# Pairing the chunk inverses, moving one page pool, and giving one chain priority in a hybrid encoder layer

## The chip, the core and the metric

The kernel runs on one core of one Trainium2 chip. It computes one layer of a streaming encoder for one sequence of 1024 frames with 1024 channels, in float32. The metric is the device time of one execution in microseconds (us). Three timed runs of the kernel before the change took 1260.48, 1262.43 and 1262.86 us; the median is 1262.43 us. A fourth execution was profiled; it took 1258.55 us, of which 1256.3 us lie between the first and the last recorded instruction.

## The reference, cut to what matters

```python
u    = rms_norm(h, mix_norm_gain)
proj = u @ w_in            # columns: attention q,k,v | delta q,k,v | gate | decay, beta
# A: band attention: 16 chunks of 64 frames, own chunk and 8 past, 8 heads of 64
q, k = rms_norm(q, q_gain), rms_norm(k, k_gain)          # per head
p    = softmax(q @ k.T * 64**-0.5 + rel_bias, masked)
o_att = rms_norm(p @ v, att_out_gain)
# B: gated delta rule: 4 heads of 128, chunks of 64 frames
t_mat = strict_lower((k*beta) @ k.T * decay) + I
value, k_cum = solve(t_mat, v*beta), solve(t_mat, k*beta*exp(decay))
for each chunk:                                          # state S is 128 x 128 per head
    v_new = value - k_cum @ S
    o     = q_decay @ S + attn_intra @ v_new
    S     = S * chunk_decay + k_tail.T @ v_new
o_dn = rms_norm(o, dn_out_gain) * silu(gate)
h = h + concat(o_att, o_dn) @ w_out
h = h + relu(rms_norm(h, ffn_gain) @ w_ff1)**2 @ w_ff2   # 1024 -> 4096 -> 1024
```

## The kernel before, in words

**Arithmetic.** Every large matrix product is made of three products of halves: an operand is split into a high part in a reduced format (`_h`) and the rest (`_l`). ScalarE (ACT) casts the high part, VectorE (DVE) or GpSimd (POOL) subtracts it (`split`, L202 to L204). The two FFN products use a Strassen-like scheme of seven products per block.

**Stages.** (1) The delta keys' projection, then the other projections in the order delta q, delta v, gate, attention keys (tiles `ak`), attention queries (`aq`), attention values (`av`); beside them runs `delta_prep`, which builds the strictly lower matrices of 8 chunks of 128 frames, sends them to DRAM (`a_dr`) and inverts their 32x32 diagonal blocks by a chain of 31 short DVE steps (L595, L599). (2) The mixer: 32 units of attention (two groups of four heads, 8 tiles of 128 frames, two pairs of heads) woven together with the delta rule. (3) The output projection (tiles `op`, `wo`). (4) `ff1`: eight blocks of seven products each (tiles `q`, L1348). (5) `ff2`: four blocks of seven products (tiles `p`, L1444).

**The attention keys' chain.** `att_proj` makes one tile of 128 frames by 24 matmuls into a PSUM bank (`ps_a`, three banks). ACT squares it (L473), DVE sums the squares (L475), then follow scale and eps (L187, DVE), a power of -0.5 (L189, POOL), one Newton step (L192, L194, L195, DVE), the row scale (L477) and the normalised tile `ak_n` (L480, DVE), which frees the bank. TensorE (PE) transposes it (L485), and it is split into `ak_h` and `ak_l`, the latter in the page pool `dk`.

**The inverses.** `delta_low` (L617) joins the 32x32 inverses to 64x64 ones for four chunks; `delta_merge` (L660) joins two 64x64 inverses of one chunk (tile `l_w`) to a 128x128 inverse (`m_yb`). It loads a 64x64 block of `a_dr` per head into `m_sa` (DMA, L667), lets POOL clear and copy parts of `m_yb` (L668 to L670), and then PE makes four 64x64 transposes (L675) and four 64x64 products (L677, eight recorded instructions), ACT copies the result to `m_sa` (L680), PE makes four more 64x64 products (L685), and ACT writes them negated to `m_yb` (L688). PSUM comes from the two banks of `ps_d`, which the whole delta rule shares. A chunk's `m_yb` is used by the product `c_pv` (L516) of `delta_state`, behind `c_pk` of the state. `delta_all` (L813) hands out the work in groups: group c holds the state step of chunk c, the output step of chunk c-1 and the merge of chunk c+2.

**What sets the order.** The mixer is written by a planner: a model clock with costs per engine decides which piece is issued next (`attention`, L831). This gives program order, which is also priority. The framework then runs the program through a model of the chip, and each engine's queue takes the ready instruction of the highest priority; inside `tc.high_priority()` an instruction goes ahead of the rest. The order found is fixed in the program. `held` (L610) issues a first matmul and makes the others follow it at high priority. On the chip every engine works through its queue in that order and waits where an operand is not there; loads are issued by SP's queue.

**Pages.** On-chip memory is cut into pools of equal pages; a tile takes a page of its pool, and when all are taken it waits until an older tile is released. In one pool, pages are handed out in the order of the program. Pool `pp` (7 pages) holds the inverses and, before the change, `m_sa`. Pool `dk` (8 pages) holds the low parts of keys and queries (`ak_l`, `aq_l`), then in program order the four key pages of the first group's first half (`ks`), the value pages `vt` 0 and 1, two key pages of the second half, later four key pages of the second group, and last the low parts of the output projection's left operand.

In the FFN the pools of `ff1` and `ff2` lie over each other: both stacks begin at the same address, and a page of `ff2` can be written once the `ff1` tiles at that address have been read for the last time. Counted in pages of 4 KB from that address, by the addresses of the program before:

| | w0 | h | l | ub11 | ub21 | ut1 | ut2 | ub22 | ut3 | ut4 | w |
|---|---|---|---|---|---|---|---|---|---|---|---|
| ff1 | 0-1 | 2-3 | 4-5 | 6-9 | 10-13 | 14-17 | 18-21 | 22-25 | 26-29 | 30-33 | 34-39 |

| | s1 | hB | r | hA | lA | rc | r2 | lB | y7 |
|---|---|---|---|---|---|---|---|---|---|
| ff2 | 0-1 | 2-5 | 6-13 | 14-17 | 18-21 | 22-27 | 28-35 | 36-39 | 40-41 |

A pool's first tile takes its first page, the second its last, the third the last but one, and so on. In `ff1`, `ub11` ... `ut4` hold the split right operands; each block multiplies them in the order b11, b21, t1, t2, b22, t3, t4; `h` and `l` hold the split left operands of the products at work, and in the last block page 4 holds the low part for t3, page 5 that for t4. In `ff2`, pool `r` holds the loads `a11` and `b11` (first product, `p1`), `rc` the loads `a21`, `a22`, `b12` (needed by the second, `p5`), `r2` those of the third; `s1` holds sums that DVE computes for `p5` (L1522); `hA`, `lA`, `hB`, `lB` hold the splits, A for the first, third, fifth product, B for the others. `p5` of the first block is at high priority.

## Time and profile before

| what | value |
|---|---|
| median of three timed runs | 1262.43 us |
| profiled execution, its own time | 1258.55 us |
| its span, first to last instruction | 1256.3 us |
| PE busy | 1236.3 us, 98% of the span |
| DVE, ACT, POOL busy | 74%, 44%, 22% |
| granted TensorE clock, mean | 0.998 |
| PE busy from 361 to 537 us, the mixer | 169.63 of 176 us |
| PE busy from 633 to 957 us, ff1 up to the first stall of ff2 | 321.22 of 324 us |

A row of the timeline gives the start, the busy time, the engine, the line of the kernel, the operation, `out<-in` by tile names without their numbers, the shapes and the count; what stands in square brackets is the idle time of the engine before it and what ended it. Consecutive instructions of one kind are put together, so "x4, 0.41" is four instructions in 0.41 us. Matmul ends are modelled and each overlaps the next, so the distance between two starts is the better measure of what a matmul occupies.

### The profile page before, as it was taken

Reading aid. Unit: us, or ns where it says so; the run is one execution under the profiler, and the core shown is the slowest. Engines: PE = TensorE matmul, PEld = TensorE weight load, DVE = VectorE, ACT = ScalarE, POOL = GpSimd, SP = SyncE. Lnnn points to the kernel's source line nnn. Section 1 sums busy time; section 2 is a strip of 40 time slices with the busy share of each in tenths; the row PEclk is TensorE's granted clock in tenths of the full one; section 3 lists DMA queues with packets and bytes.
Section 4 is the critical chain, followed back from the end, with each engine's and each line's share of the span. In section 5 each row is a group of like instructions: output and inputs, shape, how many; then the busy total and the mean of one; then the engine's idle time right before and its main releaser. Section 6 shows DMA issues by size and latency. Waiting matters only on the chain.

```text
span 1256.3 us, 17942 instructions
## 1 busy us (share of the span) xinstructions
PE 1236.3 (98%) x6686; PEld 1032.1 (82%) x6686; DVE 932.9 (74%) x1417; ACT 548.1 (44%) x899; POOL 270.5 (22%) x458
## 2 busy tenths in 40 slices
PE   9999999999999999899999999999999999999997
PEld 8778888788889988778888788888887888888886
DVE  7899987755237568776269766767769997997988
ACT  7233132232246756655365444454444543333330
POOL 4425552253133444523200000000000000000043
PEclk9999999999999999999999999999999999999999
DMA  7214364665585633045243333333269614333002
GB/s 228 63 41 141 101 164 118 119 161 134 168 259 136 189 85 88 24 135 176 76 143 104 114 118 118 119 132 101 84 205 365 202 67 134 105 97 101 1 34 100
DMA packets 134374, 158.52 MB, mean 126 GB/s; under 512 B 31120, under 2 KB 78224, under 8 KB 133776
## 3 DMA queue, kind: packets, MB, share of 16 engines
q1 hardware_dynamic: 116192, 135.11, 35.6%
q10 hardware_dynamic: 18096, 22.29, 5.2%
q8 instruction: 52, 0.85, 0.3%
q14 instruction: 34, 0.28, 0.1%
HBM read 109.91 MB, written 47.45 MB: 125 GB/s over the span
## 4 chain that ended last, share of the span: by engine, by line
PE 55%; DVE 5%; ACT 1%; issue 1%; POOL 0%; DVEq 0%; ACTq 0%
PE p L1444 24%; PE q L1348 21%; PE op L222 7%; PE t_o L1026 1%; DVE h L1290 1%; PE t_sa L927 0%; DVE q_0a_l L204 0%; PE t_tpb L987 0%; PE t_tpa L1003 0%; PE t_sb L927 0%; PE c_pv L516 0%; ACT t_pb L966 0%; PE c_po L516 0%; PE t_tpo L520 0%; PE c_pq L516 0%
## 5 line engine op out<-in xcount | busy, mean ns | idle before, releaser
L1516 POOL TENSOR_TENSOR y<-y,y 128x1024 f32<-128x1024 f32 x4 | 11.5, 2890 | 575.7 <-DVE y L1512 570.6
L1512 DVE TENSOR_TENSOR y<-y,p 128x1024 f32<-128x1024 f32 x46 | 55.1, 1217 | 5.4 <-PE p L1444 4.5
L222 PE MATMUL op<-ml,wo_h 128*128 128x512 f32 x128 | 50.2, 395 | 0.0
L222 PE MATMUL op<-mh,wo_h 128*128 128x512 f32 x128 | 49.2, 394 | 0.8 <-ACT mh L203 0.8
L222 PE MATMUL op<-mh,wo_l 128*128 128x512 f32 x128 | 49.3, 391 | 0.0
L947 DVE CUSTOM_DVE_ANT_0 t_pb<-t_sb,biasn 128x256 f32<-128x256 f32 (+1 forms) x64 | 23.2, 401 | 31.4 <-PE t_sb L927 31.3
L966 ACT ACTIVATE t_pb<-t_pb,t_nm 128x256 f32<-128x256 f32 (+1 forms) x64 | 31.4, 491 | 17.2 <-DVE t_nm L958 15.5
L1229 DVE TENSOR_TENSOR h<-op,op_x 128x512 f32<-128x512 f32 x16 | 10.8, 686 | 29.2 <-PE op L222 29.2
L1236 POOL TENSOR_TENSOR op_q<-op_q 128x512 f32<-128x512 f32 x14 | 19.6, 1400 | 55.4 <-ACT op_q L1235 55.1
L222 PEld LDWEIGHTS op<-mh,wo_h 128*128 128x128 f32 x128 | 23.9, 188 | 6.4 <-ACT mh L203 1.2
L222 PEld LDWEIGHTS op<-ml,wo_h 128*128 128x128 f32 x128 | 24.1, 188 | 5.0 <-DVE ml L204 0.2
L222 PEld LDWEIGHTS op<-mh,wo_l 128*128 128x128 f32 x128 | 24.1, 188 | 5.0
L958 DVE CUSTOM_DVE_ANT_0 t_pa<-t_sa,biaso,t_nm 128x384 f32<-128x384 f32 (+2 forms) x48 | 24.9, 543 | 2.8 <-PE t_sa L927 1.6
L970 ACT ACTIVATE t_pa<-t_pa,t_nm 128x384 f32<-128x384 f32 (+2 forms) x48 | 26.5, 552 | 0.0
L222 PE MATMUL aq_ps<-waq_h,ul 128*128 128x512 f32 x64 | 25.5, 399 | 0.0
L222 PE MATMUL dq_ps<-uh,wdq_h 128*128 128x512 f32 x64 | 25.5, 399 | 0.0
L222 PE MATMUL dv_ps<-ul,wdv_h 128*128 128x512 f32 x64 | 25.5, 399 | 0.0
L222 PE MATMUL dq_ps<-ul,wdq_h 128*128 128x512 f32 x64 | 25.3, 396 | 0.0
L222 PE MATMUL g_ps<-ul,wg_h 128*128 128x512 f32 x64 | 25.2, 394 | 0.0
L927 PE MATMUL t_sb<-ks,t_q 128*128 128x256 f32 (+1 forms) x144 | 24.0, 294 | 1.3 <-DVE t_nm L947 1.3
L222 PE MATMUL g_ps<-uh,wg_h 128*128 128x512 f32 x64 | 25.2, 394 | 0.0
L222 PE MATMUL aq_ps<-waq_h,uh 128*128 128x512 f32 x64 | 25.2, 396 | 0.0
(1109 smaller groups left out, 4304.3 us busy)
## 6 DMA issues: line engine op xcount, KB each, us to landing
wa<-in_w_ff_dram SPq DMA_DIRECT2D x32, 512.0 KB, 4.0
a<-in_w_ff_dram SPq DMA_DIRECT2D x32, 512.0 KB, 3.8
b<-f_dr SPq DMA_DIRECT2D x32, 512.0 KB, 3.4
f_dr<-yy ACTq DMA_DIRECT2D x16, 512.0 KB
t_q<-q_dr SPq DMA_DIRECT2D x30, 256.0 KB, 3.6
f_dr<-zz ACTq DMA_DIRECT2D x13, 512.0 KB
ks<-k_dr SPq DMA_DIRECT2D x16, 256.0 KB, 7.8
wo_r<-in_w_out_dram SPq DMA_DIRECT2D x16, 256.0 KB, 5.2
```

The lines of the kernel that those rows point to most:

```text
L222: nc.tensor.matmul(ps, a, b, start=(first and i == 0), stop=(last and i == n - 1))
L927: nc.tensor.matmul(o, q[m][:, i * P:(i + 1) * P], k[:, c], start=(m == 0), stop=(m == 1))
L947: nc.vector.tensor_tensor_reduce(sb[:, c], bk[:, c], new[g][pp][:, c], -1.0, 3.0e38, ALU.add, ALU.min, nm[:, 4 + i:5 + i])
L958: nc.vector.tensor_tensor_reduce(sa[e][:, 0:wa], bk[:, 0:wa], old[g][i][:, 384 - wa:384], -1.0, nm[:, 4 + i:5 + i], ALU.add, ALU.min, nm[: ...
L966: nc.scalar.activation(sb[:, c], sb[:, c], AF.Exp, bias=m, scale=-1.0, accum_out=T["sums"][:, 4 + i:5 + i])
L970: nc.scalar.activation(sa[e][:, 0:wa], sa[e][:, 0:wa], AF.Exp, bias=m, scale=-1.0, accum_out=T["sums"][:, i:i + 1])
L1026: return nc.tensor.matmul(po[64 * e:64 * e + 64, pp * P:(pp + 1) * P], vt[k0 + j][:, 64 * h:64 * h + 64], (ta[e] if j < na else tb)[:, c:c ...
L1236: nc.gpsimd.tensor_tensor(acc, acc, sq, ALU.add)
L1290: nc.vector.tensor_tensor(t, wide(R[a], i), wide(R[b], i), ALU.subtract)
L1348: nc.tensor.matmul(part(ps, q), l[:, s], r, start=(k + m == 0), stop=(k == 3 and m == 2))
L1444: nc.tensor.matmul(part(ps[q], 0) if by_rows else part(ps[q // 2], q % 2), l[:, s], part(r, k), start=(i + k + m == 0), stop=(i + k + m == 4))
L1512: nc.vector.tensor_tensor(y[i][m], y[i][m], ps[m], op)
```

## The change

It touches four functions. In `att_proj`, the chain from the scale-and-eps step to the normalised tile is put at high priority, for keys and queries. `delta_merge` now makes two chunks: both chunks' loads and POOL work first; then one run of products and transposes, the second chunk's ahead of the first's, into two PSUM banks, held together by `held`; two copies by ACT; one bank and one held run for the last products of both; two negations. Its `sa` pages come from pool `dk` in place of `pp`. `delta_all` calls it in groups 0, 2 and 4 and once ahead of them. In `ffn`, pool `s1` is listed behind `rc`, which gives in the page count above: hB 0-3, r 4-11, hA 12-15, lA 16-19, rc 20-25, s1 26-27, and r2, lB, y7 where they were.

```diff
@@ -473,13 +473,14 @@
             nc.scalar.activation(sq, ps, AF.Square, scale=r_col[:, t:t + 1])
             ss = small("a", n + "_ss", 8)
             nc.vector.tensor_reduce(ss, sq.rearrange("p (h d) -> p h d", d=ATT_D), AX.X, ALU.add)
-            r = rsqrt("a", ss, 8, 1.0 / ATT_D, EPS, n)
-            nc.vector.tensor_scalar(r, r, r_col[:, t:t + 1], None, ALU.mult)
-            qn = page("jv", n + "_n")
-            q3 = qn.rearrange("p (h d) -> p h d", d=ATT_D)
-            nc.vector.tensor_tensor(
-                q3, ps.rearrange("p (h d) -> p h d", d=ATT_D),
-                r.unsqueeze(2).broadcast_to([P, 8, ATT_D]), ALU.mult)
+            with tc.high_priority():
+                r = rsqrt("a", ss, 8, 1.0 / ATT_D, EPS, n)
+                nc.vector.tensor_scalar(r, r, r_col[:, t:t + 1], None, ALU.mult)
+                qn = page("jv", n + "_n")
+                q3 = qn.rearrange("p (h d) -> p h d", d=ATT_D)
+                nc.vector.tensor_tensor(
+                    q3, ps.rearrange("p (h d) -> p h d", d=ATT_D),
+                    r.unsqueeze(2).broadcast_to([P, 8, ATT_D]), ALU.mult)
             tp = bank(ps_t, n + "_tp")
             for i in range(4):
                 nc.tensor.transpose(tp[:, i * P:(i + 1) * P], qn[:, i * P:(i + 1) * P], ident)
@@ -659,35 +660,54 @@
 
     def delta_merge(c, W, res):
 
+
         n = f"m{c}"
-        Yp, sa = page("pp", n + "_yb"), page("pp", n + "_sa")
-        Y = b4(Yp)
-        A = sa[:, 0:256].rearrange("p (h e) -> p h e", h=4)
-        Yd = W[c // 2].rearrange("p (c h e) -> p c h e", c=2, h=4)[:, c % 2]
-        nc.sync.dma_start(out=A[64:128], in_=a_dr[:, c].rearrange("r (h e) -> r h e", h=4)[64:128, :, 0:64])
-        nc.gpsimd.memset(Y[64:128, :, 0:64], 0.0)
-        nc.gpsimd.tensor_copy(Y[0:64, :, 0:64], Yd[0:64])
-        nc.gpsimd.tensor_copy(Y[64:128, :, 64:128], Yd[64:128])
-        on("g", 1700)
+        pair = range(2)
+        Yp = [page("pp", f"{n}_yb{i}") for i in pair]
+        sa = [page("dk", f"{n}_sa{i}") for i in pair]
+        Y = [b4(t) for t in Yp]
+        A = [t[:, 0:256].rearrange("p (h e) -> p h e", h=4) for t in sa]
+        Yd = W[c // 2].rearrange("p (c h e) -> p c h e", c=2, h=4)
+        for i in pair:
+            nc.sync.dma_start(out=A[i][64:128],
+                              in_=a_dr[:, c + i].rearrange("r (h e) -> r h e", h=4)[64:128, :, 0:64])
+            nc.gpsimd.memset(Y[i][64:128, :, 0:64], 0.0)
+            nc.gpsimd.tensor_copy(Y[i][0:64, :, 0:64], Yd[0:64, i])
+            nc.gpsimd.tensor_copy(Y[i][64:128, :, 64:128], Yd[64:128, i])
+        on("g", 3400)
         yield max(clock.now + 5000, when.get(("low", c // 4), 0)), "d"
-        tp = bank(ps_d, n + "_tp")
-        for h in range(4):
-            nc.tensor.transpose(tp[0:64, h * 64:h * 64 + 64], Yd[0:64, h, :], ident[0:64, 0:64])
-        for h in range(4):
-            nc.tensor.matmul(tp[0:64, 256 + h * 64:320 + h * 64], A[64:128, h, :], Yd[64:128, h, :],
-                             start=True, stop=True)
+        tp = [bank(ps_d, f"{n}_tp{i}") for i in pair]
+
+        def step(i, h, turned):
+            hs = slice(h * 64, h * 64 + 64)
+            if turned:
+                return nc.tensor.transpose(tp[i][0:64, hs], Yd[0:64, i, h, :], ident[0:64, 0:64])
+            return nc.tensor.matmul(tp[i][0:64, 256 + h * 64:320 + h * 64], A[i][64:128, h, :], Yd[64:128, i, h, :],
+                                    start=True, stop=True)
+
+        held([(i, h, turned) for i in (1, 0) for turned in (False, True) for h in range(4)], step)
         with tc.high_priority():
-            nc.scalar.copy(sa[0:64, :], tp[0:64, :])
-        yield give("d", on("s", 577, pe(900), ahead=True)), "d"
+            for i in (1, 0):
+                nc.scalar.copy(sa[i][0:64, :], tp[i][0:64, :])
+        t = pe(1800)
+        give("d", on("s", 577, t, ahead=True))
+        yield give("d", on("s", 577, t, ahead=True)), "d"
         p4 = bank(ps_d, n + "_p4")
-        for h in range(4):
+
+        def last(i, h):
             hs = slice(h * 64, h * 64 + 64)
-            nc.tensor.matmul(p4[0:64, hs], sa[0:64, hs], sa[0:64, 256 + h * 64:320 + h * 64],
-                             start=True, stop=True)
+            return nc.tensor.matmul(p4[0:64, i * 256 + h * 64:i * 256 + h * 64 + 64], sa[i][0:64, hs],
+                                    sa[i][0:64, 256 + h * 64:320 + h * 64], start=True, stop=True)
+
+        held([(i, h) for i in (0, 1) for h in range(4)], last)
         with tc.high_priority():
-            nc.scalar.mul(Y[0:64, :, 64:128], p4[0:64, 0:256].rearrange("p (h e) -> p h e", h=4), -1.0)
-        res[c] = Yp
-        when["Y", c] = give("d", on("s", 375, pe(600), ahead=True))
+            for i in pair:
+                nc.scalar.mul(Y[i][0:64, :, 64:128],
+                              p4[0:64, i * 256:i * 256 + 256].rearrange("p (h e) -> p h e", h=4), -1.0)
+        t = give("d", on("s", 750, pe(1200), ahead=True))
+        for i in pair:
+            res[c + i] = Yp[i]
+            when["Y", c + i] = t
 
     def delta_state(c, ab, kTs, Ys, D):
 
@@ -813,14 +833,14 @@
     def delta_all(ab, kTs, W):
 
         Ys, D = {}, {}
-        yield dict(M=chained(delta_merge(0, W, Ys), delta_merge(1, W, Ys)))
+        yield dict(M=delta_merge(0, W, Ys))
         for c in range(NT + LATE):
             gens = {}
             if c < NT:
                 gens["S"] = delta_state(c, ab, kTs, Ys, D)
             if 0 < c <= NT:
                 gens["O"] = delta_out(c - 1, ab, kTs, D)
-            if c + 2 < NT:
+            if c % 2 == 0 and c + 2 < NT:
                 gens["M"] = delta_merge(c + 2, W, Ys)
                 if c == 2:
                     gens["M"] = chained(delta_low(1, W, "wh"), gens["M"])
@@ -1588,7 +1608,7 @@
             with ExitStack() as st1:
                 ff1(R, begun, psw, stage(st1, "ff1", {"w0": 2, "h": 2, "l": 2, "ub11": 4, "ub21": 4, "ut1": 4, "ut2": 4,
                                                "ub22": 4, "ut3": 4, "ut4": 4, "w": 6, "h2": 1, "l2": 1, "r2": 1}))
-            ff2(psw, stage(st, "ff2", {"s1": 2, "hB": 4, "r": 8, "hA": 4, "lA": 4, "rc": 6, "r2": 8, "lB": 4, "y7": 2}))
+            ff2(psw, stage(st, "ff2", {"hB": 4, "r": 8, "hA": 4, "lA": 4, "rc": 6, "s1": 2, "r2": 8, "lB": 4, "y7": 2}))
 
     def first_steps(gen, n):
         for _ in range(n):
```

## The prediction

> **What bounds the kernel now.** The page's first part comes first, then PE's waits, then the windows of the stages that the change touches.
>
> ```profile
> PE 1236.3 (98%) x6686; PEld 1032.1 (82%) x6686; DVE 932.9 (74%) x1417; ACT 548.1 (44%) x899; POOL 270.5 (22%) x458
> ...
> PE ak_tp L485 <- DVE ak_n L480: 1.9, 1, 1.9
> PE p L1444 <- DVE p50b_l L204: 1.8, 1, 1.8
> ...
> 361.00:471.00 110.00, 109.12 (x1144) 1.00 0.57 158
> 471.00:537.00 66.00, 60.51 (x575) 1.00 0.20 57
> ```
>
> PE is busy for 1236.3 us of the span of 1256.3, so waits taken away can bring 20.0 us at the very most; more can come only from PE time that is itself saved. The two longest waits (us in total, times, longest) are the change's: the keys' transpose waits 1.9 us for the normalised tile, and ff2's second product 1.8 us for its split. The mixer has two parts: up to 471 us PE idles 0.9 of 110 us, and what it saves there is saved; from 471 to 537 it idles 5.5 of 66 us, so chains over DVE and ACT share in setting the end.
>
> **The keys' chain.** DVE's and PE's timeline at the first tile of keys:
>
> ```profile
> 227.29 0.17 DVE L192 TENSOR_TENSOR ak_t<-ak_y 128x8 f32<-128x8 f32 x1
> 228.04 0.68 DVE L475 TENSOR_REDUCE ak_ss<-ak_sq 128x8 f32<-128x512 f32 x1
> 229.25 0.68 DVE L480 TENSOR_TENSOR ak_n<-ak_ps,ak_r 128x512 f32<-128x512 f32 x1
> 229.99 0.66 PE L485 MATMUL ak_tp<-ident,ak_n 128*128 128x128 f32 x4 [1.88 <-DVE ak_n L480]
> ...
> 240.01 0.17 DVE L192 TENSOR_TENSOR ak_t<-ak_y 128x8 f32<-128x8 f32 x1 [1.75 <-POOL ak_y L189]
> 240.88 0.69 DVE L480 TENSOR_TENSOR ak_n<-ak_ps,ak_r 128x512 f32<-128x512 f32 x1
> ```
>
> From the Newton step's start to the normalised tile's start the first tile needs 229.25 - 227.29 = 1.96 us; a later tile, with nothing in between, 240.88 - 240.01 = 0.87 us. In between stand steps of the block inversion and the next tile's sum (L475, 0.68 us). Priority can take 1.09 us out. It may take less: the steps depend on each other, and the build fills such a gap with a ready instruction of any priority, as between every two steps here. The sum of squares itself stays outside the priority. Ends: 0 and the whole 1.88 us; I take **-0.9**, the distance to the undisturbed tile less one small filler. The inversion steps that move back by as much are followed by loads, not by PE work; PE's next need is the second tile, which comes behind 24 matmuls. If that cover were gone, at most the 1.09 us would come back.
>
> **The merges: PE time.** PE's timeline around them (64x64 instructions among 128x128 ones):
>
> ```profile
> 282.48 0.41 PE L675 MATMUL m_tp<-ident,l_w 64*64 64x64 f32 x4
> ...
> 315.69 0.39 PE L222 MATMUL av_ps<-wav_h,ul 128*128 128x512 f32 x1
> 315.92 0.39 PE L222 MATMUL av_ps<-wav_h,uh 128*128 128x512 f32 x1
> 316.24 0.56 PE L677 MATMUL m_tp<-l_w,m_sa 64*64 64x64 f32 x6
> 316.73 0.50 PE L222 MATMUL av_ps<-wav_l,uh 128*128 128x512 f32 x1
> ...
> 418.23 0.41 PE L675 MATMUL m_tp<-ident,l_w 64*64 64x64 f32 x4
> 418.57 0.67 PE L677 MATMUL m_tp<-l_w,m_sa 64*64 64x64 f32 x8
> 419.18 0.68 PE L927 MATMUL t_sa<-ks,t_q 128*128 128x256 f32 x4
> ...
> 469.67 0.68 PE L685 MATMUL m_p<-m_sa 64*64 64x64 f32 x8
> ```
>
> No instruction is removed: both kernels transpose and multiply the same blocks. What changes is how often PE turns from 128x128 to 64x64 and back. A 512-wide matmul occupies 315.92 - 315.69 = 0.23 us, but the first 64x64 one starts 0.32 us behind its predecessor: entering costs 0.09. From first start to the next foreign start, six instructions take 0.49 us, eight 0.61: 0.06 each and 0.13 fixed. So a group costs **0.22 us** beside its work. Between the first and the last row above the timeline has 21 such groups: five for chunk 0, four for chunk 5 (its last products are cut in three), two for each of the others. The change needs two for each of four pairs, 8 if `held` keeps them whole: 13 x 0.22 = 2.9 us less. Against it stands the alternation inside a group: products (from rows 64 to 127) and transposes (rows 0 to 63) turn 12 times in place of 7. Four transposes take 0.34 us, 0.10 more than 4 x 0.06, so five turns cost 0.5. That leaves **2.4 us** of PE time. [...]
>
> How much reaches the end: all groups lie before 471 us, where PE idles 0.9 of 110 us, so 2.4 us arrive there; behind it the chains decide with PE. Ends: 0 and -2.4. I take **-1.5**, nearer to the second, as 92% of that part is PE too.
>
> **The merges: new waits.** `m_sa` moves to the pool `dk`, whose pages go out in program order. Loads, copies and users of the tiles concerned:
>
> ```profile
> 252.86 1.28 SPq L667 DMA_DIRECT2D m_sa<-a_dr  x2
> 349.82 0.30 POOL L866 COPY vt<-av_s 128x1 f32<-128x1 f32 x2
> 356.50 1.89 SPq L860 DMA_DIRECT2D ks<-k_dr  x4
> 363.29 0.56 ACT L680 COPY m_sa<-m_tp 64x512 f32<-64x512 f32 x1
> 366.18 1.13 PE L516 MATMUL c_pv<-c_jv,m_yb 128*128 128x128 f32 x8
> 381.18 0.67 PE L685 MATMUL m_p<-m_sa 64*64 64x64 f32 x8
> 384.94 0.42 DVE L947 CUSTOM_DVE_ANT_0 t_pb<-t_sb,biasn 128x256 f32<-128x256 f32 x1 [0.15 <-PE t_sb L927]
> 432.24 1.07 PE L927 MATMUL t_sa<-ks,t_q 128*128 128x128 f32 x8
> 448.97 0.91 PE L516 MATMUL c_pv<-c_jv,m_yb 128*128 128x128 f32 x6
> ...
> DMA to landing us min/median/max: 3.6/4.0/6.2
> ...
> DMA to landing us min/median/max: 7.8/7.8/7.8
> ```
>
> The last two rows are the landings of `m_sa` and of `ks`. In the changed program the first pair's pages come behind `vt` 0 and 1, so at 349.8 us and not at 253; behind the loads queued on SP, issue is at about 352. With 4.0 to 6.2 us of landing, 2.0 of products and transposes (two times 0.95), 1.2 of two copies, 1.2 of last products (two times 0.61) and 0.8 of negations (0.4 each, an estimate from the copy's 0.56, as they are half as wide) the inverses are there at 361.2 to 363.4; the first `c_pv` starts at 366.18. The second pair gets pages when the first releases them, about 361.5, and releases them at 370 to 374 by the same terms. Only then do two key pages of the second half come, in place of 356.5; landed at 378 to 382, they are used at about 384.3, just ahead of the 384.94 row. The third pair waits until tile 7 of the first group has read its keys (432.24 + 1.07): 433.3 + 0.4 + 4.0 to 6.2 + 5.2 gives 442.9 to 445.1, against 448.97. All three fit, with 2.3 us at the tightest: cost **0** in the sum, its price below. A load that waits for a page on SP holds the queue's later loads, the queries' among them. POOL's and ACT's instructions are as many as before; both `ps_d` banks are taken for about 3.2 us per pair, while the state steps shown by `c_pv` lie some 20 us apart.
>
> **The last stage's pages.** SP's, ACT's, DVE's and PE's timelines at the turn from ff1 to ff2:
>
> ```profile
> 907.74 5.58 SPq L1479 DMA_DIRECT2D a<-in_w_ff_dram  x2
> 929.50 9.33 SPq L1479 DMA_DIRECT2D a<-in_w_ff_dram  x4
> 930.19 1.22 DVE L204 TENSOR_TENSOR p10a_l<-a,p10a_h 128x1024 fp32r<-128x1024 f32 x1
> 937.24 0.39 PE L1348 MATMUL q<-t3h,q_7a_l 128*128 128x512 f32 x1
> 937.47 0.39 PE L1348 MATMUL q<-t4h,q_7a_h 128*128 128x512 f32 x1
> 937.92 0.39 PE L1444 MATMUL p<-p10b_h,p10a_h 128*128 128x512 f32 x1
> 941.15 1.06 ACT L1353 ACTIVATE yy<-yy 128x1024 f32<-128x1024 f32 x1
> 956.18 0.50 PE L1444 MATMUL p<-p50b_l,p50a_h 128*128 128x512 f32 x1 [1.78 <-DVE p50b_l L204]
> ...
> DMA to landing us min/median/max: 3.7/3.8/11.4
> ```
>
> `rc` moves from pages 22-27 to 20-25: its loads no longer need t3's pages, and the four that ran from 929.5 to 938.8 us can all go by the end of b22, about 932. DVE's preparation of the second product starts some 6 us earlier, and the 1.78 us wait goes. But `r` moves too: its first tile, the first `a11`, falls from page 6 (free at 907.7) on page 4, which t3's products read until 937.24 + 0.39 = 937.6. Its load (last row: 3.8 us) lands at 941.4; ACT is busy until 942.2, its cast takes as long as that row (1.06) and DVE's subtraction 1.22: high part at 943.3, low part at 944.6. PE ends t4 at 937.47 + 24 x 0.23 = 943.0, since the seven instructions of `p1` that filled in from 937.92 no longer can; `p1` starts at 943.3, and its third matmul, due at 943.75, waits for 944.6: 1.2 us. Net **-0.6**. Ends: -1.8 with no wait left, and a landing of 11.4 us (the row's maximum), which gives +6.2.
>
> **Sum**: -0.9 - 1.5 - 0.6 = -3.0 us. The profiled execution took 1258.55 us, 3.9 below the timed median, so it would take 1255.5 and the median 1262.43 - 3.0 = **1259.4**.
>
> **Rivals.** (1) The mixer's end is bound by its chains and gives the PE time back: -1.5 us, 1260.9. For it: 5.5 us idle behind 471; against it: PE is 92% busy there. (2) Slower: the second pair releases its pages late. The point is 384.3 - 7.8 - 0.4 = 376.1 us. If its last products run where chunk 3's did (381.18 to 381.85), the keys land at 390.0, 5.7 us late; with all of it on PE's path the sum is 5.7 - 3.0 = +2.7, 1265.1. For it: 2.3 us of slack over a chain of ten steps; against it: PE has other work meanwhile. (3) The first `a11` lands after 11.4 us: +6.2 - 2.4 = +3.8, 1266.2. For it: the DMA engines fill up from 940 us on; against it: a load at 937.7 is ahead of that, and the second product's loads are gone by then. (4) The priority changes nothing and the groups are cut as before: -0.6, 1261.8.
>
> **Numbers.** The forecast has 0.45 (own range 1256 to 1260.6), rival 1 0.25, rival 2 0.13, rival 3 0.12, rival 4 0.05. A measurement of this kernel can tell 0.2% from no change, that is 2.5 us: 1259.9 to 1265.0. Faster has 0.38 of the forecast and 0.05 of rival 1; slower has rivals 2 and 3 nearly whole: 0.43, 0.33, 0.24. The range reaches from the forecast with all gains (-1.9 - 2.4 - 1.8 = -6.1, 1256.3, and 1.3 for a shifted order) to rival 3 and as much above: 1255 to 1267.
>
> **What would show it.** Keys: the 1.88 us wait ahead of L485 falls to about 1. Merges: eight groups of 64x64 instructions, each whole; `ks` loads at about 375 us without PE idle at 384. ff2: no wait for p50b, a wait of about 1.2 us for `p10a_l` instead. Wrong would be: more idle PE time between 361 and 537 us than 6.4, or a wait over 1.8 us at `p1`.

## The result, and the profile after

Six timed runs of the changed kernel have a median of 1293.8 us (1288.9 to 1297.3), six of the kernel before on the same chip 1261.9 us (1260.0 to 1262.9): 1.025 times as long, 95% interval 1.023 to 1.028. The forecast was 1259.4. The profiled execution took 1292.1 us, its span is 1290.2, and the mean granted clock 0.985 in place of 0.998.

The changed kernel's lines stand 1 to 20 further down: L667 is now L672, L675 L684, L677 L685, L685 L699, L516 L517, L1348 L1368, L1444 L1464. The page of the changed kernel, engines and PE's waits (us in total, times, longest):

```profile
PE 1248.7 (97%) x6686; PEld 1041.3 (81%) x6686; DVE 941.4 (73%) x1415; ACT 547.4 (42%) x901; POOL 268.2 (21%) x458
...
PE m_tp L685 <- DMA m_sa<-a_dr: 6.1, 2, 3.5
PE p L1464 <- ACT p10b_h L203: 5.5, 1, 5.5
PE p L1464 <- DVE p10b_l L204: 2.8, 1, 2.8
PE ak_tp L486 <- DVE ak_n L481: 2.3, 1, 2.3
```

Each part of the change has a wait here, and two are new: the merges' products wait for the load of `m_sa`, ff2's first product for its splits. By PE's timeline the last matmul of the value projection ends at 361.0 us (360.3 before), that of the output projection at 654.7 (632.9), of ff1 at 966.9 (944.7), of ff2 at 1283.8 (1249.8). So mixer and output projection take 293.6 us in place of 272.6, **+21.0**; ff1 +0.5; ff2 316.9 in place of 305.2, **+11.7**. The waits in the rows above, 16.7 us, are half of the 33.9 us that the span grew by. Both signs that the prediction named for being wrong are there: PE is idle for 14.7 us between 361 and 537 us, not 6.4, and the wait at `p1` is over 1.8.

The mixer, on SP's and PE's timelines of the changed kernel (here and below rows are picked from the timelines, and what lies between them is left out):

```profile
364.32 1.26 SPq L672 DMA_DIRECT2D m_sa<-a_dr  x2
370.80 1.09 PE L685 MATMUL m_tp<-l_w,m_sa 64*64 64x64 f32 x8 [3.54 <-DMA m_sa<-a_dr]
...
416.89 1.05 PE L517 MATMUL c_po<-c_vn,c_att 128*128 128x128 f32 x8
433.80 1.29 SPq L672 DMA_DIRECT2D m_sa<-a_dr  x2
439.15 0.67 PE L685 MATMUL m_tp<-l_w,m_sa 64*64 64x64 f32 x8 [2.53 <-DMA m_sa<-a_dr]
444.69 1.97 PE L699 MATMUL m_p<-m_sa 64*64 64x64 f32 x16
452.91 0.60 PE L521 MATMUL c_tpv<-ident,c_jv 128*128 128x128 f32 x4
458.04 1.06 PE L517 MATMUL c_pv<-c_jv,m_yb 128*128 128x128 f32 x8
```

and the same steps of the delta rule in the kernel before:

```profile
421.78 0.60 PE L520 MATMUL c_tpv<-ident,c_jv 128*128 128x128 f32 x4
427.97 1.16 PE L516 MATMUL c_pv<-c_jv,m_yb 128*128 128x128 f32 x8
```

The third pair's load goes out at 433.8, as forecast (433.7). What the forecast didn't see stands around it: from the end of `c_po` at 417.9 to 439.2 PE has no matmul of the delta rule at all, and chunk 3's state step, which began with `c_tpv` at 421.78 and reached `c_pv` at 427.97, now begins at 452.91 and reaches it at 458.04, 30 us later. PE stands still for only some 4 of these 21 us, 2.5 of them for the load; it does attention meanwhile. Over mixer and output projection its idle time is 18.8 us in place of 7.1. That is 11.7 of the 21.0 us; the other 9.3 are busy time, though no work was added, at a mean granted clock of 0.95 (see the point on the clock below).

ff2's first product, SP, ACT, DVE and PE:

```profile
961.45 1.24 SPq L1499 DMA_DIRECT2D a<-in_w_ff_dram  x2
962.73 1.26 SPq L1499 DMA_DIRECT2D b<-f_dr  x2
966.47 0.39 PE L1368 MATMUL q<-t4h,q_7a_l 128*128 128x512 f32 x1
968.42 1.06 ACT L1372 ACTIVATE yy<-yy 128x1024 f32<-128x1024 f32 x1 [1.49 <-DVE yy L1422]
969.38 1.03 ACT L203 CAST p10a_h<-a 128x1024 fp32r<-128x1024 f32 x1
970.32 1.05 ACT L1373 ACTIVATE yy<-yy 128x1024 f32<-128x1024 f32 x1
971.28 1.03 ACT L203 CAST p10b_h<-b 128x1024 fp32r<-128x1024 f32 x1
972.36 1.22 PE L1464 MATMUL p<-p10b_h,p10a_h 128*128 128x512 f32 x2 [5.50 <-ACT p10b_h L203]
976.39 0.80 PE L1464 MATMUL p<-p10b_l,p10a_h 128*128 128x512 f32 x1 [2.81 <-DVE p10b_l L204]
976.98 0.63 PE L1464 MATMUL p<-p10b_h,p10a_l 128*128 128x512 f32 x1
977.41 0.63 PE L1464 MATMUL p<-p10b_h,p10a_h 128*128 128x512 f32 x1
```

All four loads of the first product go out behind t3's last read (961.4), not only the first; their casts stand on ACT among ff1's last squares (L1372, L1373), and PE's last ff1 matmul starts at 966.47. The last two rows show something that no part of the forecast had: consecutive 512-wide matmuls start 0.43 us apart, not 0.23.

### The profile page after: what moved, and what is told of

It is laid out like the page before. It is cut to its first block, busy times and chain, and to the rows that moved or that the text cites. A ratio compares the mean times of both kernels' runs of the same rounds, so it can differ in the third digit from the quotient of the medians.

```text
span 1290.2 us, 17930 instructions
## 1 busy us (share of the span) xinstructions
PE 1248.7 (97%) x6686; PEld 1041.3 (81%) x6686; DVE 941.4 (73%) x1415; ACT 547.4 (42%) x901; POOL 268.2 (21%) x458
## 4 chain that ended last, share of the span: by engine, by line
PE 83%; DVE 8%; DMA 5%; issue 1%; ACT 1%; POOL 1%; SPq 1%; ACTq 0%; DVEq 0%; POOLq 0%
PE p L1464 22%; PE q L1368 20%; PE op L222 7%; PE av_ps L222 3%; PE dq_ps L222 3%; PE aq_ps L222 3%; PE dv_ps L222 3%; PE dk_ps L362 2%; PE ak_ps L222 2%; PE t_o L1046 2%; PE g_ps L222 2%; PE t_sb L947 1%; PE t_sa L947 1%; PE t_tpb L1007 1%; DMA m_sa<-a_dr 1%
## 5 line engine op out<-in xcount | busy, mean ns | idle before, releaser
L1536 POOL TENSOR_TENSOR y<-y,y 128x1024 f32<-128x1024 f32 x4 | 11.5, 2899 | 587.9 <-DVE y L1532 582.8
L986 ACT ACTIVATE t_pb<-t_pb,t_nm 128x256 f32<-128x256 f32 (+1 forms) x64 | 31.3, 490 | 14.9 <-DVE t_nm L978 11.9
L222 PEld LDWEIGHTS op<-mh,wo_l 128*128 128x128 f32 x128 | 24.2, 189 | 5.0
L1376 DVE TENSOR_TENSOR zz<-zz,r 128x1024 f32<-128x1024 f32 x13 | 15.9, 1225 | 14.2 <-ACT zz L1373 14.2
L222 PE MATMUL av_ps<-wav_l,uh 128*128 128x512 f32 x64 | 25.2, 394 | 0.0
```

The lines of the kernel that those rows point to most:

```text
L222: nc.tensor.matmul(ps, a, b, start=(first and i == 0), stop=(last and i == n - 1))
L986: nc.scalar.activation(sb[:, c], sb[:, c], AF.Exp, bias=m, scale=-1.0, accum_out=T["sums"][:, 4 + i:5 + i])
L1376: nc.vector.tensor_tensor(two(t), two(t), r2[:, th:th + 1, :].broadcast_to([P, 2, TH]), ALU.mult)
```

## The experiments

Each ratio is to the kernel before, run on the same chip with it.

**The three parts, one at a time.** `keys_only` has the first hunk of the change, `ff2_only` the last, `merge_only` the two in the middle.

> The kernel before with the keys' priority alone. Theory: the priority does not move a step at the first tile of keys, because between two dependent steps of the chain the build puts any ready DVE instruction, and the sum of squares of the next tile (0.68 us) and two inversion steps are ready there; the wait ahead of the keys' transposes stays at 1.9 to 2.4 us, and the time is that of before within 1 us (1261 to 1263). Rival: the chain does get shorter by itself, and only the other parts of the change hid that; then the wait falls to about 1 us and the time to 1260 to 1261.

> The kernel before with the new order of ff2's pools alone. Theory (one late page holds the queue): all four loads of the first product stand behind the first a11 on SP's queue and land after ff1's last product; PE waits about 5.5 and 2.8 us at p1, the granted clock falls to half for about 8 us behind it, which costs 4 us more, and the 1.8 us wait at p5 goes: 1272 to 1275. Rival (the stall came from the changed mixer, whose later end shifts the loads against ff1's last writes): no wait over 2 us at p1 and 1260 to 1263.

> The kernel before with the paired merges alone, their loaded pages in pool dk as in the change. Theory (pages come late and PE's queue stands): the two waits ahead of the merges' products are there (about 3.5 and 2.5 us), later ones of 1 to 2 us follow, the granted clock falls below 0.9 in the slices behind the longer ones, and the whole mixer loses 19 to 22 us: 1281 to 1284. Rival (a good part of the mixer's loss comes from the order that the keys' and queries' priority left in dk): under 1275.

| kernel | median, us | before, us | ratio, 95% interval | mixer and output projection, us | ff2, us |
|---|---|---|---|---|---|
| keys_only | 1261.5 | 1261.2 | 1.0002 (0.9991 to 1.0013) | 273.3 | 305.1 |
| ff2_only | 1270.3 | 1261.2 | 1.0068 (1.0049 to 1.0088) | 272.9 | 316.9 |
| merge_only | 1285.4 | 1261.2 | 1.0188 (1.0166 to 1.0210) | 293.3 | 305.1 |

The parts add up: 0.3 + 9.1 + 24.2 = 33.6 us, against 31.9 for all three. The stage totals of the table agree with the changed kernel's, part by part (ff1, which it leaves out, takes 311.8 us before, 312.2 in the changed kernel, 310.2 to 314.9 in the three). For ff2 and the merges the waits are about those of the theories (5.5 and 2.8 us at `p1`, 3.2 and 2.3 us ahead of the merges' products) and the rivals fall, though `ff2_only` takes 2 to 5 us less than its theory said, and `merge_only` 1 us more. For the keys the theory holds too. DVE's and PE's timelines of `keys_only`:

```profile
228.40 0.17 DVE L192 TENSOR_TENSOR ak_t<-ak_y 128x8 f32<-128x8 f32 x1
229.14 0.68 DVE L475 TENSOR_REDUCE ak_ss<-ak_sq 128x8 f32<-128x512 f32 x1
230.36 0.68 DVE L481 TENSOR_TENSOR ak_n<-ak_ps,ak_r 128x512 f32<-128x512 f32 x1
231.10 1.11 PE L486 MATMUL ak_tp<-ident,ak_n 128*128 128x128 f32 x4 [3.21 <-DVE ak_n L481]
```

With the priority the chain takes 230.36 - 228.40 = 1.96 us, exactly as before, and the next tile's sum still stands in it. The wait is 3.21 us here; in executions without the priority it was 1.76 to 3.21 us, so its size in one profile says nothing.

**Pages or pairing?** `merge_pp` is `merge_only` with `sa` back in `pp`; `sa_dk` is the kernel before, with its single merges, and `sa` in `dk`.

```diff
-        sa = [page("dk", f"{n}_sa{i}") for i in pair]
+        sa = [page("pp", f"{n}_sa{i}") for i in pair]
```

> The paired merges alone, with their loaded pages in pool pp, where the kernel before has them. Theory (the pages of dk are the cause): the loads go out early, no wait of PE ahead of the merges' products stays over 1 us, the granted clock stays at 1.00 in the mixer, and what is left is the saved switching: 1258 to 1261. Rival (pairing itself is the cause, a held run of 16 instructions in two banks of the delta rule's PSUM makes the state steps wait): 1270 or more, with the waits at the state's tiles (c_) and not at the merges'.

> The kernel before, its merges one chunk at a time as they were, but with the loaded pages of the merges taken from pool dk. Theory (the late page is the cause by itself, pairing only adds to it): loads of m_sa go out some 100 us later than before, PE waits ahead of the merges' products or of c_pv, and the mixer gets at least 8 us longer: 1269 or more. Rival (it takes the pair, which wants two pages at once and holds 24 instructions behind one load): within 3 us of before, 1259 to 1264.

`merge_pp`: 1263.7 us, 1.0018 (1.0006 to 1.0029). `sa_dk`: 1278.8 against 1262.1, 1.0130 (1.0113 to 1.0146). So the page pool makes the loss, with pairs or without. Pairing by itself costs about 2 us (0.8 to 3.7) where the expectation had a gain. PE's and SP's timelines of `sa_dk`:

```profile
416.22 0.58 SPq L667 DMA_DIRECT2D m_sa<-a_dr  x1
419.44 0.68 PE L677 MATMUL m_tp<-l_w,m_sa 64*64 64x64 f32 x8
422.67 1.16 PE L516 MATMUL c_pv<-c_jv,m_yb 128*128 128x128 f32 x8
...
557.29 1.12 PE L987 MATMUL t_tpb<-ident,t_pb 128*128 128x128 f32 x4 [8.18 <-ACT t_ta L1008]
```

PE doesn't wait for this load at all (it waits 2.3 us for a load of queries at 373), and the mixer is 19.0 us longer: chunk 1's `c_pv`, at 381.78 before, stands until 422.67, and the idle time appears at the mixer's end, 8.18 us in one piece at 549 to 557, before an instruction of attention. The waits named beside a late load are not its price.

What the pairing itself saves can be read in `merge_pp`: 11 groups of 64x64 instructions (8 in the forecast; the build cut three first runs in two) in place of 21, occupying 11.9 us in place of 13.0; with 0.09 for each of the ten entries less that is 2.0 us of PE time (2.4 forecast). None of it arrives. Mixer and output projection as one window (length, then busy time of PE, its weight loads, DVE, ACT, POOL, the clock, DMA), before and in `merge_pp`:

```profile
360.30:632.90 272.60, 265.48 (x2183) 232.36 (x2184) 171.30 (x474) 159.39 (x426) 107.44 (x245) 1.00 0.42 122
```

```profile
365.50:639.80 274.30, 262.78 (x2157) 228.81 (x2155) 173.78 (x472) 157.83 (x425) 107.27 (x239) 1.00 0.43 123
```

PE is busy for 2.7 us less and idle for 4.4 us more.

**Which pair?** `pair2_dk` and `pair3_dk` are `merge_pp` with one pair's pages in `dk`; `merge_odd` is `merge_only` with each pair made one group later.

```diff
-        sa = [page("dk", f"{n}_sa{i}") for i in pair]
+        sa = [page("dk" if c == 4 else "pp", f"{n}_sa{i}") for i in pair]
...
-            if c % 2 == 0 and c + 2 < NT:
-                gens["M"] = delta_merge(c + 2, W, Ys)
+            if c % 2 and c + 1 < NT:
+                gens["M"] = delta_merge(c + 1, W, Ys)
```

> The same with only the second pair (chunks 2 and 3) in dk. There PE's wait ahead of the merge's product is the longest of the mixer (3.2 to 3.5 us), but the state step behind it is late by only some 6 us. Theory (state chain): the rest of the chain is on time and takes the delay up, and the mixer gets 0 to 7 us longer: 1263 to 1270, with the long wait of PE there all the same. Rival (PE's waits and the clock decide): here the loss is the larger of the two, more than with the third pair.

> Paired merges with their loaded pages in pool pp, save the third pair (chunks 4 and 5), whose two stay in dk. Theory (state chain): the third pair's bank tiles stand in program order ahead of chunk 3's state step and take both banks of ps_d until the load lands, which waits for the page that the first group's last tile reads at about 435 us; no matmul of the delta rule runs for some 20 us, c_pv of chunk 3 starts 20 us or more later than with all pages in pp, and the mixer gets 15 to 21 us longer, though PE's own waits at this place stay under 3 us: 1278 to 1284. Rival (the sum of PE's waits and of the low clock behind them): 2.5 us of wait and some 2 us for the clock, 1266 to 1269.

> Paired merges with all loaded pages in dk, as in the change, but each pair one group later: with the state steps of chunks 1, 3 and 5 in place of 0, 2 and 4. The pages come free and the loads go out when they do in the change; what moves is the order in which the banks of ps_d are asked for. Theory (state chain held by banks): chunk 3's state step no longer stands behind the third pair, its c_pv starts at 425 to 440 us, and at least half of the 20.7 us of the mixer comes back: 1262 to 1273. Rival (the late load itself is the cost, whoever stands behind it): chunk 4's own step is late in its turn and the mixer stays at least 15 us longer: 1277 or more.

`pair2_dk`: 1263.9 us, 1.0019 (1.0006 to 1.0032), as `merge_pp`; the long wait that was expected there isn't, since with the first pair in `pp` the second pair's loads go out at 356.0 us. `pair3_dk`: 1275.0, 1.0094 (1.0061 to 1.0127), with one run of 1267 among three of 1275 to 1276, which is below the theory's 1278 to 1284 and above the rival's 1266 to 1269. The profile is of the run of 1267. In it chunk 3's `c_pv` starts at 448.7 in place of 431.3 and the last one at 528.3 in place of 515.7 (`merge_pp`), but the mixer is only 3.5 us longer than there: a late state step isn't worth its lateness. The first and the fourth pair weren't tried alone, so of `merge_only`'s 24 us the third pair by itself explains 11 to 13, the second none, and for the rest no pair is shown. `merge_odd`: 1268.6, 1.0059 (1.0038 to 1.0080): 17 of `merge_only`'s 24 us are back with the loads as late as ever, though chunk 3's `c_pv` came at 450.5, not at 425 to 440: the pair still slipped in between two products of that step. So the time came out as the theory had it, but not by its mechanism. In its profile the mixer is 10.6 us shorter than in `merge_only`; 8.6 of that is PE's busy time, at a clock of 0.99 in place of 0.95, and 2.0 its idle time.

**What holds the state step?** `pair3_banks` is `pair3_dk` with the third pair's first banks from the pool `ps_t`, which attention's transposes use, in place of `ps_d`; `pair3_out` takes the bank of its last products there too.

```diff
-        tp = [bank(ps_d, f"{n}_tp{i}") for i in pair]
+        tp = [bank(ps_t if c == 4 else ps_d, f"{n}_tp{i}") for i in pair]
...
-        p4 = bank(ps_d, n + "_p4")
+        p4 = bank(ps_t if c == 4 else ps_d, n + "_p4")
```

> As pair3_dk (only the third pair's loaded pages in dk), but the two banks into which the third pair multiplies come from ps_t, which the attention's transposes use, in place of ps_d. Load and page are as late as in pair3_dk. Theory (the state step stands behind the merge because both banks of ps_d are taken): the state step of chunk 3 goes on while the merge waits, its c_pv starts at 428 to 438 us as with all pages in pp (431.3), in place of 448.7, and the last c_pv at 515 to 520 in place of 528.3; the attention pays for the lent banks, so the time is only said to be below pair3_dk's median of 1275. Rival (the late load or PE's queue holds the step): c_pv of chunk 3 stays at 445 us or later.

> As pair3_banks, and the bank of the third pair's last products (m_p) comes from ps_t too, so that no tile of this pair stands in ps_d's order. Its load is as late as before. Theory (banks of ps_d are handed out in program order, and a tile of the pair that is not yet needed holds those of the next state step, be there a free bank or not; in pair3_banks that was the tile of the last products): now the state step of chunk 3 goes on while the merge waits, its c_pv starts at 428 to 438 us in place of 444.5. Rival (the order of PE's queue, which the build made, holds it: the pair's matmuls stand ahead of the step's whatever banks they use): c_pv of chunk 3 starts at 443 us or later, and no delta matmul runs between about 411 and 430 us.

The theory that both banks are occupied fell with `pair3_banks`: the state step was late all the same. PE's timeline there, and in `pair3_out`:

```profile
430.20 0.68 PE L684 MATMUL m_tp<-l_w,m_sa 64*64 64x64 f32 x8 [2.46 <-DMA m_sa<-a_dr]
433.50 1.97 PE L698 MATMUL m_p<-m_sa 64*64 64x64 f32 x16
438.23 0.67 PE L520 MATMUL c_tpv<-ident,c_jv 128*128 128x128 f32 x4
444.54 1.05 PE L516 MATMUL c_pv<-c_jv,m_yb 128*128 128x128 f32 x8
```

```profile
421.25 0.60 PE L520 MATMUL c_tpv<-ident,c_jv 128*128 128x128 f32 x4
425.12 0.49 PE L1022 MATMUL t_tpa<-ident,t_pa 128*128 128x128 f32 x3
425.45 1.06 PE L516 MATMUL c_pv<-c_jv,m_yb 128*128 128x128 f32 x8
437.63 1.12 PE L684 MATMUL m_tp<-l_w,m_sa 64*64 64x64 f32 x8 [2.63 <-DMA m_sa<-a_dr]
444.74 1.11 PE L1006 MATMUL t_tpb<-ident,t_pb 128*128 128x128 f32 x4
513.31 1.16 PE L516 MATMUL c_pv<-c_jv,m_yb 128*128 128x128 f32 x8 [0.38 <-DVE c_jv L739]
```

Once no tile of the pair stands in that pool's order, the step goes by at 421 to 425 us, ahead of a load that is as late as before, and the last `c_pv` is at 513.3 as with no late page (515.7 in `merge_pp`). Chunk 3's `c_pv`, at 425.45, is a little ahead of the expected 428 to 438, and the rival of 443 or later falls. So a pool gives out its banks in program order: one tile not yet wanted (`m_p`, waiting for copies that wait for the load) keeps every later tile back, even with the pair's first two tiles elsewhere. On the chip this shows as the order of PE's queue, which the build fixed: where the step is late, PE has its matmuls behind the pair's, and its one wait of over 1 us there is for the load. The time doesn't follow: `pair3_banks` takes 1277.4 us, 1.0132 (1.0115 to 1.0149), and `pair3_out` 1272.7 against 1261.5, 1.0081 (1.0059 to 1.0103). Attention's pool now has the late tiles in its order, and its transposes stand behind them: in `pair3_out` there is none from 425.6 (`t_tpa`) to 444.7 us (`t_tpb`), 19.1 us, where the longest such pause in `merge_pp` up to 537 us is 7.8. What that pause costs isn't shown: PE is idle in the mixer for 11.2 us in `pair3_out` and for 11.5 in `merge_pp`, and what grew is its busy time, by 6.5 us, at a clock of 0.98 (behind the wait of 2.63 us come 10 us at half clock). `pair3_banks` as a whole is slower than `pair3_dk`, which its expectation had ruled out.

**ff2: which page?** `rc_early`, `rc_mid` and `r_kept` are the kernel before with other orders of ff2's pools; `ff2_skip` is `ff2_only` with a tile that nobody reads put first into pool `r`.

```diff
-{"s1": 2, "hB": 4, "r": 8, "hA": 4, "lA": 4, "rc": 6, "r2": 8, "lB": 4, "y7": 2}
+{"hB": 4, "y7": 2, "r": 8, "hA": 4, "lA": 4, "rc": 6, "s1": 2, "r2": 8, "lB": 4}   r_kept
+{"hB": 4, "y7": 2, "r": 8, "rc": 6, "hA": 4, "lA": 4, "s1": 2, "r2": 8, "lB": 4}   rc_early
+{"s1": 2, "hB": 4, "r": 8, "hA": 4, "rc": 6, "lA": 4, "r2": 8, "lB": 4, "y7": 2}   rc_mid
```

> The kernel before with ff2's pools in the order hB, y7, r, hA, lA, rc, s1, r2, lB: the sums' pool s1 lies behind rc as in the change, but r, hA, lA and rc stay on the pages of before (6 to 13, 14 to 17, 18 to 21, 22 to 27). Theory (the loss in ff2 is r's first page, two pages further down): no wait at p1, the wait of 1.8 us at p5 as before, ff2 as long as before: 1260.5 to 1262.5. Rival (s1 behind rc, or hB on pages 0 to 3, which stay in use longest, delays the second product): p5 waits longer than 1.8 us and 1264 or more.

> The new order of ff2's pools alone, with one tile that nobody reads put on the first page of pool r (page 4, free last); the four loads of the first product fall on pages 11 to 8, free 30 us earlier. It does no work of the reference. Theory (one late page at the head of SP's queue made the whole loss in ff2): p1 doesn't wait over 1 us, ff2 is as long as before or up to 2 us shorter since rc still comes early: 1259.5 to 1262.5. Rival (the loads of rc, which now go ahead of the queue, and the seven others fill the DMA engines, and the stall only moves to p5): 1266 or more.

> The kernel before with another order of ff2's pools: hB, y7, r, rc, hA, lA, s1, r2, lB. Pool r is back on pages 6 to 13, free early; rc moves to 14 to 19, hA to 20 to 23, lA to 24 to 27, s1 to 28 and 29. Theory (a late page of r was the whole loss of the change in ff2, and earlier pages for rc are worth the p5 wait): no wait at p1, none or a shorter one for p50b_l, ff2 1 to 2 us shorter than before: 1259.5 to 1260.5. Rival (the wait at p5 is set by DVE's order and not by the loads, or the splits wait for hA and lA): p5 waits 1.8 us as before or p1 waits over 1 us, 1261 to 1265.

> The kernel before with rc on pages 18 to 23 and lA on 24 to 27, all else as before (order s1, hB, r, hA, rc, lA, r2, lB, y7). Theory (rc's loads are what p5 waits for): rc comes some 5 us earlier, the p5 wait goes and nothing else waits instead, 1 to 1.8 us less: 1259.5 to 1261. Rival (the low parts of the first product now wait for lA's pages, as with rc_early): p1 waits about 1 us and nothing is gained: 1261 to 1263.5.

`r_kept`: 1261.5 us, 1.0004 (0.9993 to 1.0015), no wait at `p1`. Moving `s1` behind `rc` is free (`r2` and `lB` lie two pages further up with it); with `r` on its old pages the loss is gone, here and in `rc_early` and `rc_mid`, where `rc` comes early. `ff2_skip` was meant to show the same and went the other way, 1277.1, 1.0120 (1.0101 to 1.0140): by the addresses of the program the extra tile put the first load on page 11 and pushed the second to page 5, which t4 reads until 946 us; the expectation had the four loads on pages 11 to 8. SP's, POOL's, ACT's and PE's timelines there:

```profile
940.81 5.81 SPq L1479 DMA_DIRECT2D a<-in_w_ff_dram  x3
940.85 0.10 POOL L1494 MEMSET empty<- 128x1 f32 x1 [301.91 <-PE q L1348]
946.66 1.13 SPq L1479 DMA_DIRECT2D b<-f_dr  x2
960.61 1.04 ACT L203 CAST p10b_h<-b 128x1024 fp32r<-128x1024 f32 x1 [9.75 <-DMA b<-f_dr]
961.71 1.22 PE L1444 MATMUL p<-p10b_h,p10a_h 128*128 128x512 f32 x2 [15.49 <-ACT p10b_h L203]
```

The empty tile gets page 4 at 940.85, by POOL, not by SP's queue, and the first load, whose page 11 had been free since t1's products began some 22 us earlier, goes out only then; the loads of `b` follow when page 5 is free. It is the pool's order again: a late page at its head makes all behind it late. The loads were slow as well, which its rival had in part: from the issue of `b` to the end of the wait for it, 960.6, it is some 14 us, with the DMA engines 96% busy. What each of the two costs isn't separated. `rc_early`, 1.0009 (0.9998 to 1.0020), and `rc_mid`, 1.0004 (0.9991 to 1.0017), both took the 1.8 us wait at `p5` away and got others: `rc_early` 1.1 us at `p1` and 1.2 later, `rc_mid` 2.3 us at 957 to 959, behind ACT's copy of sums. Nothing is gained, as the rivals had it; for `rc_mid` the place was another than its rival's `p1`.

**What the low clock costs.** `clock_gaps` measures it by itself; `ff2_fill` is `ff2_only` with PE kept busy where it waits.

```diff
+                if name == "p10" and i == 0:
+                    for _ in range(24):
+                        nc.tensor.matmul(part(ps[1], 1)[:, 0:P], ones, ones, start=True, stop=True)
+                    for _ in range(9):
+                        nc.tensor.matmul(part(ps[1], 1), ops[0][0][0][:, 0:P], part(ops[0][1][0], 0), start=True, stop=True)
```

> A kernel of its own that computes nothing of the reference: 20 groups of 48 matmuls (128x512, some 11 us each), and between two groups a chain of 2 to 16 copies on ScalarE that the next group waits for, so that PE stands still for some 1 to 9 us. Theory (a standstill over a bound makes the granted clock fall): groups behind waits below 2 us run at 0.23 us per matmul from the first one, groups behind waits over 5 us begin at 0.43 us per matmul for several us, and between the two it happens to some groups and not to others. Rival (the low clock in the changed kernel was not a matter of PE's waits): all groups begin at 0.23 us, or all at 0.43.

> The new order of ff2's pools alone, with matmuls whose result is overwritten put into PE's queue ahead of p1: 24 of 128x128 of constants (0.17 us each) and 9 of 128x512 (0.23 us each) that need the first two high parts. They do no work of the reference; they keep PE busy while p1 waits. Theory (the half clock behind the waits comes from PE standing still and costs 4 us by itself): with no standstill over 2 us the granted clock stays at 1.00, and though p1 starts no earlier the time is 3 to 4.5 us below that of the pools alone: 1266 to 1267.5. Rival (the low clock has another cause, such as the DMA burst at this place): the clock falls all the same and the time stays at 1269 to 1272.

PE's timeline of `clock_gaps`, three of the groups of 48:

```profile
47.99 11.22 PE L35 MATMUL g<-rhs,op 128*128 128x512 f32 x48 [2.66 <-ACT op L41]
62.53 12.82 PE L35 MATMUL g<-rhs,op 128*128 128x512 f32 x48 [3.32 <-ACT op L41]
282.88 14.05 PE L35 MATMUL g<-rhs,op 128*128 128x512 f32 x48 [5.30 <-ACT op L41]
```

After waits of 1.3 to 2.7 us a group takes 11.2 us (four of five; 12.8 after one of 2.0); after all 14 waits of 3.3 to 10.6 us it takes 12.5 to 14.1, on average 2.0 us more. In `ff2_fill` the granted clock stays at 1.00 throughout ff2 (0.54 from 950 to 960 us in `ff2_only`), and the time is 1271.6, 1.0076 (1.0061 to 1.0091): nothing comes back. The clock did stay up, so the rival falls; what the theory had wrong is the price. PE's timelines of `ff2_fill` and of `ff2_only` at the second product:

```profile
962.84 0.73 PE L1444 MATMUL p<-p50b_h,p50a_h 128*128 128x512 f32 x2 [2.15 <-ACT p50b_h L203]
```

```profile
963.35 0.62 PE L1444 MATMUL p<-p50b_h,p50a_h 128*128 128x512 f32 x2
```

At full clock PE is through with the first product sooner and waits 2.15 us for `p50b_h`, whose loads are late too. The low clock had cost 0.5 us here, not 4.

**Can the keys' wait be removed?** `keys_ahead` has no priority; it writes a tile's matmuls two tiles ahead of its transposes.

```diff
-            ps = proj_N(u[t // TPH], w, t % TPH, n + "_ps")
+            for a in range(len(made), min(NT, t + 1 + (0 if kind == "v" else 2))):
+                made.append(proj_N(u[a // TPH], w, a % TPH, f"a{kind}{a}_ps"))
+            ps = made[t]
```

> The kernel before, without any priority for the keys' chain, but the 24 matmuls of a tile of keys or queries are written two tiles ahead of its transposes, so that the third tile's matmuls stand ahead of the first tile's transposes in PE's queue. Theory (the wait is the chain's length and goes only if PE has other work ahead): the wait of 1.9 to 3.2 us ahead of the first transposes goes, and with it the 0.5 us that they take longer at the low clock: 1258 to 1260. Rival (the third tile's bank is not free earlier, or the queue's order is the build's own): the wait stays and the time is that of before within 1 us.

1262.8 us against 1260.6, 1.0017 (1.0006 to 1.0028); the wait is 1.81 us, so the theory falls, but the time is 2.3 us longer, which the rival didn't have either. The edit changed nothing in this place, since the third tile was ahead already: in the kernel before, as here, 72 matmuls of `ak_ps`, three tiles of 24, stand in PE's queue ahead of the first transposes. The pool `ps_a` has three banks, and the first comes free with the normalised tile, so a fourth tile can't go ahead; more banks weren't tried. No version beat the kernel before.

## Why the prediction was wrong, point by point

**The merges' new waits: wrong, some 24 of the 32 us.** The arrival times were nearly right: first pair issued at 350.9 (352 forecast), third at 433.8 (433.7), second at 364.3 (361.5). The failed step is the comparison that followed. The third pair was held against 448.97, the `c_pv` of its own chunk, and the cost put at 0; but the delta rule's work of the same pool comes behind the pair in program order, and first in that line stood chunk 3's `c_tpv`, due at 421.78. The sentence "both `ps_d` banks are taken for about 3.2 us per pair, while the state steps shown by `c_pv` lie some 20 us apart" counted how long the matmuls take; the order was blocked from 417.9 to 439.2 and beyond. That this order delays the step is shown (`pair3_out`), and that the move of the pages makes the loss is, too (`merge_only` against `merge_pp`). How the one makes the other is shown in part only: the third pair by itself costs 11 to 13 us. Against 421.78 the forecast's own arrival times, 442.9 to 445.1, would have given 21 to 23 us of lateness; it was 31 at that step. That the mixer's 21.0 us match is partly chance, since 9.3 of them are busy time of PE.

**The second pair** came out as the rival (2) had it, with the two key loads behind it at 378.5 us, beyond its point of 376.1, but its price was wrong: in `pair2_dk` they go out at 377.0 and 378.0, as late, and nothing is lost.

**The merges' PE time: near in size, wrong in arrival.** 2.0 us saved against 2.4, with 11 groups against 8; of the 1.5 us expected at the end, nothing. "PE is 92% busy there" is no measure of what arrives; rival (1) was right in this step.

**ff2: wrong, 9 us.** The step "Its load (last row: 3.8 us) lands at 941.4", with one cast and one subtraction behind it, took one tile for four. The rest of pool `r` waits in line behind it (`ff2_skip`), and the casts behind ff1's last squares on ACT: `p1` waits 5.5 + 2.8 us in place of 1.2. Rival (3) had the place and the sign, not the reason. The forecast that the wait at `p5` goes was right. The prediction says of SP's queue that a waiting load holds the later ones, and used it for the queries, not here.

**The keys: no effect.** -0.9 was the failed term; the sentence beside it, that the build fills such a gap with a ready instruction of any priority, was the whole truth.

**The clock: not considered.** The longest wait in the profiled execution before was 1.88 us, and its windows of the mixer all show 1.00, so nothing there pointed to it, and the forecast's own waits, about 1 us at the keys and 1.2 us at `p1`, were no longer. It turned out to cost 0.5 us where it could be tested. In the mixer more of PE's time goes with it. The same windows as above, for `merge_only`, `sa_dk` and `merge_odd`:

```profile
363.70:657.00 293.30, 274.87 (x2173) 240.57 (x2172) 177.20 (x472) 158.33 (x427) 104.03 (x237) 0.95 0.39 113
362.30:653.90 291.60, 270.62 (x2186) 234.95 (x2184) 170.19 (x474) 159.64 (x426) 106.65 (x238) 0.98 0.40 116
362.70:645.40 282.70, 266.30 (x2174) 232.13 (x2173) 170.95 (x478) 155.87 (x422) 102.77 (x237) 0.99 0.41 120
```

For about the same instructions, PE is busy 9.4 us longer than before in `merge_only` and idle for 11.3 more; in `sa_dk` it is 5.1 and 13.9. So busy time at low clock is near half of the first loss and a quarter of the second. How much of it would come back at full clock isn't settled, as no kernel kept PE busy in the mixer's waits, and in ff2 nothing came back. How the rest divides between the state chain and attention isn't settled either, as `pair3_out` still loses 11 us with the chain on time.

## What to carry to other kernels

In these runs a tile's page or bank was late when the last reader of whoever had it was late, and then everything behind it in that pool's program order was late, whether it needed that page or not (`ff2_skip`: a first load at 940.8 us, though its page had been free for some 22 us; `pair3_out` against `pair3_banks`: chunk 3's `c_pv` at 425.5 us in place of 444.5). So for a moved tile list not its own consumer but the next tiles of every pool that its work passes through, and compare the arrival with the earliest of them. A wait that the profile names beside a late load can be a small part of its price, or none of it (`sa_dk`: no wait at the load of 416.2 us, and a mixer 19.0 us longer), and the PE time saved in the mixer, whose chains go on to its end, came back as idle time (`merge_pp`: 2.7 us less busy, 4.4 us more idle).

## What the runs showed of the hardware

After PE stood still, its matmuls started 0.43 us apart in place of 0.23 for some microseconds: in the changed kernel the granted clock was 0.52 from 970 to 980 us.

```profile
970.00:980.00 10.00, 4.83 (x11) 3.34 (x12) 9.74 (x9) 4.20 (x5) 0.00 (x0) 0.52 1.04 393
```

In `clock_gaps` such a stretch followed all 14 waits of 3.3 to 10.6 us and one of four waits of 2.0 to 2.7 us. Of the changed kernel's waits the one of 2.53 us was followed by it (from 441.4 us, 2.3 us behind the wait), the one of 2.33 us ahead of `ak_tp` was not. Nor do waits of one length agree: behind the wait of 1.79 us at ff2's second product the matmuls started 0.43 us apart from 959.3 to 962.3 us in `r_kept`, and behind the same wait of 1.78 us in the kernel before they stayed 0.23 apart, at a clock of 1.00. So below 3.3 us the length of a wait didn't tell in these runs whether the clock would fall. The changed kernel's trace has five such stretches up to its last matmul; windows of 6.75, 10.15, 3.35, 6.75 and 10.15 us lie inside them with the clock at 0.50 throughout:

```profile
369.75:376.50 6.75, 5.70 (x37) 5.15 (x37) 0.51 (x2) 1.74 (x3) 0.31 (x1) 0.50 1.06 242
441.45:451.60 10.15, 10.15 (x71) 9.58 (x71) 1.51 (x7) 4.17 (x15) 0.00 (x0) 0.50 0.37 91
496.05:499.40 3.35, 3.24 (x15) 3.11 (x15) 3.12 (x11) 2.51 (x9) 2.11 (x7) 0.50 0.03 7
550.65:557.40 6.75, 6.04 (x23) 5.17 (x23) 6.20 (x11) 5.35 (x12) 5.47 (x10) 0.50 0.38 118
970.50:980.65 10.15, 5.48 (x12) 3.90 (x13) 9.24 (x9) 3.70 (x4) 0.00 (x0) 0.50 1.04 396
```

A group behind one of the 14 waits took 1.3 to 2.8 us of PE time more than the 11.2 us of a fast one in `clock_gaps`; in ff2 the low clock cost 0.5 us at the second product, and with the clock at 1.00 nothing of the kernel's time came back (1270.3 us in `ff2_only`, 1271.6 in `ff2_fill`), as that product then waits 2.15 us for `p50b_h`.
